# Two layers of a diffusion backbone: sums of token halves moved from the attention's plan behind the first downward blocks, and the first downward tiles split when buffers come free

## The chip, the cores and the metric

The kernel runs on one core of one Trainium2 chip. The metric is the device time of one execution in microseconds. Before the change the median of three runs is 1696.11 us (1695.55 to 1698.88). The engines are named as in the profile: PE is TensorE, DVE is VectorE, ACT is ScalarE, POOL is GpSimd, SP is SyncE, which here issues the weight loads.

## The reference

One inference step of a diffusion backbone: two layers over 128 context tokens and 512 latent tokens (640 in all), width 1024, MLP width 4096. Each layer has an attention part and an MLP part; the change touches the seam between the two.

```python
def rmsnorm(x, g):
    xf = x.astype(jnp.float32)
    y = xf * lax.rsqrt(jnp.mean(xf * xf, axis=-1, keepdims=True) + EPS)
    return (y * g.astype(jnp.float32)).astype(x.dtype)
...
    mix = jnp.concatenate([da_o.reshape(B, S, -1), sw_o.reshape(B, S, -1), mla_o.reshape(B, S, -1)], axis=-1)
    x = x + g1 * (mix @ lw['w_out'])
    h2 = rmsnorm(x, lw['norm2_g']) * (1 + sc2) + sh2
    x = x + g2 * (jnp.square(jax.nn.relu(h2 @ lw['w_up'])) @ lw['w_down'])
    return x, state
```

The four lines from `mix` on close one layer; `mix` joins the outputs of three groups of attention heads. `h2 @ w_up` is the upward projection, the product with `w_down` the downward one. Everything is float32.

## The kernel before, in words

**Precision.** Each operand of a product is kept as a high and a low part in a narrower type that PE reads: `wh` and `wl` for weights, `hh` and `hl` for the normed activations h, `Gt` (both parts in one tile) for the squared relu. The high part is a copy (ACT, L401 or L416), the low part a subtraction of that copy from the raw value (L409, on DVE). A product is three matmuls (L544, L545, L546 in `mm3`; L1483 and L1873 where they are written out): high by high, high by low, low by high. A raw weight tile is `wr`; making `wh` and `wl` from it is called a split.

**Tokens** are worked on in two parts, `hf`=0 (256 tokens: context and the first latents) and `hf`=1 (the other 384).

**The attention plan.** All of the attention and the start of the MLP are tasks of a planner (`Plan`): each has an engine, an estimated length, what it reads and writes, ring buffers to allocate, and a priority (a smaller number goes first). The planner puts the tasks of every engine in a fixed order; on the chip an engine runs its own list in order and waits by semaphores. Rings `wh` and `wl` have four buffers each.

**The end of the plan** in each layer is:
- `emit_h`: h of the second norm, by token part and k (8 pieces of 128 features); `rb` (L681) is a small matmul that spreads the norm's factor over the partitions ahead of it. The value h before its split stays in two tiles `hs` (k 0 to 3 and k 4 to 7).
- `wino_tokens` (L1529): for each token part four subtractions `hs<-hs` of token halves and feature halves, which leave sums of blocks of h in `hs`, then their split into `Th` and `Tl`. These are operands of a scheme of seven products in place of eight that the upward projections use later. The tasks have priority 0.45e6+20; the `Th` copy may go to ACT or DVE as the planner likes ('AV').
- `first_up` (L1473): the upward projection of the first four f-blocks (f=0..3, 128 columns of w_up each). For `hf`=0 (L1483) and then for `hf`=1 (L544 to L546, 384 wide) it loops over k, and within k over all four f. Each f uses one buffer of the rings `wh` and `wl` to its end. Then relu on ACT (L1468), its square on DVE (L1469, named `r`), and the split into `Gt`.
- `pre`: loads and splits of the first two downward tiles, d0 and d1, of priority 3.5e6+4, so their buffers are the ones of f=0 and 1.

**The MLP** behind the plan is written out by hand. `downs(0)` gives eight blocks: for each of four w_down tiles (d0 to d3) one block for `hf`=0 and one for `hf`=1, of 24 matmuls each. Each accumulates in two PSUM banks, which DVE adds to the residual x (L747 in `emit_resid`: 128 wide twice for `hf`=0, 384 wide for `hf`=1). `ups(1)` follows: fourteen blocks (L1873), for two pairs of f-blocks (f=4 and f=6) the seven products A11, A12, S2, S3, S1, A22, S4 in that order; A11, A12 and S4 take h itself, the others `Th` and `Tl`. Their weights are sums of raw tiles that POOL makes (`wr<-wr`, `ws<-wr` at L409, and `pool_late`, L1784).

**What feeds the blocks.** `prep()` splits the next weight tile as soon as the block that used its ring slot last has been issued; it stands at the end of the loop over blocks. Tiles 4 to 7 (two products each: A11 and A12 of f=4; S2 and S3; S1 and A22; then S4 of f=4 with A11 of f=6) are prepared behind blocks 1, 3, 5 and 7. `advance()` then issues the next raw loads on SP: there are four raw buffers, and one is loaded anew once the tiles that read it have been split. When the second raw tile of a pair is there, POOL makes its sums.

```python
                for f_ in now + late:
                    f_()
                late = later
                while state["tile"] < len(tiles) and last_use[state["tile"] - RINGS["wh"]] <= b_:
                    prep()
```

Here `now` holds what empties the PSUM banks of this block, `late` the split of the previous block's `r` into `Gt`.

Of the kernel before, what the change touches and what calls it, by code (L numbers as in the profile page):

```python
# [10 lines left out]
F32 = mybir.dt.float32  # L11
# [47 lines left out]
N_PRE = 2  # L59
# [307 lines left out]
def tile_hybrid_step(ctx: ExitStack, tc: tile.TileContext, i, o):  # L367
    nc = tc.nc
    V, S, G, T = nc.vector, nc.scalar, nc.gpsimd, nc.tensor
# [12 lines left out]
    def mk(ring, shape, dt=F32, name=None):  # L382
        tag = SHARE.get(ring, ring)

        def make():
            pool = psum[ring] if ring in psum else pool_of.get(tag, mp)
            return pool.tile(shape, dt, tag=tag, name=name or ring, bufs=N_RAW if tag == "wr" else RINGS[tag])
        s = Slot(ring, make)
        s.name = name or ring
        return s  # L390

    def add(*a, **k):
        return cur[0].add(*a, **k)
# [5 lines left out]
    def copy(eng, out, in_):  # L399
        if eng is S:  # L400
            S.activation(out=out, in_=in_, func=AF.Copy)  # L401
        else:
            eng.tensor_copy(out, in_)
# [4 lines left out]
    def sub(eng, out, a, b):  # L408
        eng.tensor_tensor(out=out, in0=a, in1=b, op=ALU.subtract)  # L409
# [27 lines left out]
    def sl(t, table, key):  # L437
# [30 lines left out]
                    in1=sil[:, 2].rearrange("p (k s) -> p k s", s=2), op=ALU.mult)  # L468
# [61 lines left out]
    def load_split(src, n, prio, k=1, load_prio=None, after=(), sb=None):  # L530

        raw = load(src, n, prio if load_prio is None else load_prio, after)
        hi, lo = mk("wh", [P, 1024], R), mk("wl", [P, 1024], R)
        split(n, lambda: hi.t[:, :n], lambda: lo.t[:, :n], lambda: raw.t[:, :n], [raw], (hi, lo), prio,
              hi_alloc=[hi], lo_alloc=[lo], sb=sb or PAR["weights"], extra=0.05)

        def view():
            return tuple(s.t[:, :n].rearrange("p (k n) -> p k n", k=k) for s in (hi, lo))

        return view, [hi, lo]  # L540
# [931 lines left out]

    def first_up(l, h, Gt, ws, after):  # L1473

        acc = mk("s", [P, 4, 256], F32, "pu")
        add("V", tV(1024), lambda: V.memset(acc.t, 0.0), alloc=[acc], prio=0.35e6, after=after)
        for k in range(KD):
            for f in range(4):
                def mm(k=k, f=f):
                    wh, wl = ws[f][0]()  # L1480
                    hh, hl = (h_at(h, x, k, slice(*HALVES[0])) for x in "hl")
                    for w, a in ((wh, hh), (wh, hl), (wl, hh)):
                        T.matmul(out=acc.t[:, f], lhsT=w[:, k], rhs=a, start=False, stop=k == KD - 1 and w is wl,  # L1483
                                 skip_group_check=True)

                add("P", 3 * tP(256), mm, r=h_rd(h, k, 0) + ws[f][1], w=[(acc, f)], prio=1.2e6 + 0.1 * k + 0.01 * f)
        acc1 = mk("s", [P, 2, 512], F32, "pu")
        pus = [mk("t", [P, 384], F32, "pu") for _ in range(2)]
        late = [((acc1, f), lambda f=f: acc1.t[:, f, 0:384]) for f in range(2)] + [(x, lambda x=x: x.t) for x in pus]
        for k in range(KD):  # L1490
            for f in range(4):
                key, out = late[f]

                def mm(k=k, f=f, out=out):
                    wh, wl = ws[f][0]()
                    mm3(out(), (wh[:, k], wl[:, k]), [h_at(h, x, k, slice(*HALVES[1])) for x in "hl"], k == 0, k == KD - 1)

                al = [] if k else [[acc1], [], [pus[0]], [pus[1]]][f]
                add("P", 3 * tP(384), mm, r=h_rd(h, k, 1) + ws[f][1], w=[] if al else [key], alloc=al,
                    prio=1.2e6 + 1 + 0.1 * k + 0.01 * f)  # L1500
        for hf in range(2):
            for f in range(4):
                a0, b0 = HALVES[hf]
                w = b0 - a0
                r = mk("E", [P, NT], F32, "r")
                gt = Gt[f // 2]
                d = {}
                pu, out = late[f] if hf else ((acc, f), lambda f=f: acc.t[:, f])

                def stage(x, d=d, gt=gt, f=f, hf=hf, out=out, r=r):  # L1510
                    if "s" not in d:
                        d["s"] = up_out(gt.t, f, hf, out(), r.t)
                    d["s"][x]()

                pr = 0.4e6 + 500 + 4 * hf + f
                add("A", tA(w), lambda stage=stage: stage(0), r=[pu], alloc=[r], prio=pr)
                add("V", tV(w), lambda stage=stage: stage(1), r=[pu], w=[r], prio=pr)
                add("A", tA(w) + 0.05, lambda stage=stage: stage(2), r=[r], w=[(gt, ("h", f, hf))], prio=pr)
                add("V", tV(w), lambda stage=stage: stage(3), r=[r, (gt, ("h", f, hf))], w=[(gt, ("l", f, hf))], prio=pr)
# [4 lines left out]
    def half(ap, x):  # L1524

        return ap.rearrange("p k (t a n) -> p k t a n", a=2, n=64)[:, :, :, x] if len(ap.shape) == 3 else \
            ap.rearrange("p (t a n) -> p t a n", a=2, n=64)[:, :, x]

    def wino_tokens(hs, Tl, Th):  # L1529

        for hf in range(2):
            a, b = HALVES[hf]
            w = (b - a) * 2
            every = [(hs[x], (4 * x + k, hf)) for x in range(2) for k in range(4)]

            def v(s, x, a=a, b=b):
                return half(hs[s].t[:, :, a:b], x)

            for out, in0, in1 in (((0, 0), (0, 1), (0, 0)), ((0, 1), (1, 1), (0, 1)),
                                  ((1, 1), (1, 1), (0, 0)), ((1, 0), (1, 0), (1, 1))):  # L1540
                add("V", tV(w), lambda e=V, v=v, out=out, in0=in0, in1=in1: sub(
                    e, v(*out), v(*in0), v(*in1)), r=every, w=every, prio=0.45e6 + 20)
            for x in (1, 0):
                c = (slice(None), slice(4 * x, 4 * x + 4), slice(a, b))
                n = 4 * (b - a)
                kk = [(4 * x + k, hf) for k in range(4)]
                src = [(hs[x], q) for q in kk]
                sv = lambda x=x, a=a, b=b: hs[x].t[:, :, a:b]
                add("AV", {"A": tA(n), "V": tV2(n)}, lambda e, c=c, sv=sv: copy(e, Th.t[c], sv()),
                    r=src, w=[(Th, q) for q in kk], prio=0.45e6 + 20)  # L1550
                add("V", tV(n), lambda e=V, c=c, sv=sv: sub(e, Tl.t[c], sv(), Th.t[c].bitcast(F32)),
                    r=[(Th, q) for q in kk] + src, w=[(Tl, q) for q in kk], prio=0.45e6 + 20)


    def last_down(l, dn, Gt, st):
# [42 lines left out]
    for l in range(DEPTH + 1):  # L1598
        with ExitStack() as es:
# [17 lines left out]
            if l == 0:  # L1617
                st = open_stats("z")
                for k2 in range(4):
                    add("D", 2 * P * NT * 4 / DMAR, lambda k2=k2: dma(xT[:, 2 * k2:2 * k2 + 2], i["xT"][:, 2 * k2:2 * k2 + 2]),  # L1620
                        w=[("x", (k, hf)) for k in (2 * k2, 2 * k2 + 1) for hf in range(2)], prio=0.0)
# [12 lines left out]
            if l == DEPTH:  # L1634
                for hf in (1, 0):
                    a, b = HALVES[hf]
                    for k in range(KD):
                        def fy(hf=hf, k=k, a=a, b=b):
# [4 lines left out]
                            r=[("x", (k, hf))], prio=0.0)  # L1643
# [21 lines left out]
            for tok in PAR["seq"].split():  # L1665
                kind, u = tok[0], int(tok[1:])
                if kind == "c":
                    for _ in range(u):
                        c = next(conds, None)
# [13 lines left out]
                else:  # L1683
                    n = count[tok] = count.get(tok, -1) + 1
# [22 lines left out]
            Tl, Th = (mk("T", [P, KD, NT], R, n) for n in ("Tl", "Th"))  # L1707
            for x in (Tl, Th):
                x.keep = True
            add("V", 0.0, lambda: None, alloc=[Tl, Th], prio=0.0, after=[gate["mla"]])  # L1710
            hs = [mk("hs", [P, 4, NT], F32, "hs") for _ in range(2)]
            add("V", 0.0, lambda: None, alloc=hs, prio=0.0, after=[gate["mla"]])
            rb2s = rstds(st2, ("o", "t"), 0.3e6, False)
            for hf in range(2):
                for k in range(KD):
                    emit_h(l, 1, hf, rb2s[hf], h2, k, 0.3e6 + 20 * hf + k, hs)
            wino_tokens(hs, Tl, Th)
            upw = []
            for f in range(4):
                upw.append(load_split(i["w_up"][l, f], 1024, PAR["up_prio"] + f, 8, sb=PAR["up"], load_prio=3.5e6 + f))  # L1720
# [12 lines left out]
        with ExitStack() as es:  # L1733
# [10 lines left out]
            Tlt, Tht = Tl.t, Th.t  # L1744
# [91 lines left out]
                return [half(t[:, 4 * x[1]:4 * x[1] + 4], x[2]) for t in (Tht, Tlt)]  # L1836

            banks, late = {}, []
            advance()
            while state["tile"] < RINGS["wh"]:  # L1840
                prep()
            for b_, blk in enumerate(blocks):
                kind, f, q, x, n_ = blk
                wh, wl = wt[n_]
                now, later = [], []
                if kind == "d":
                    g, mc, hf = f, q, x
# [11 lines left out]
                else:  # L1859
# [10 lines left out]
                    out = pu.rearrange("p (t n) -> p t n", n=64)  # L1870
# [4 lines left out]
                    if q in ("A11", "S2", "S3"):  # L1875
                        e = mp.tile([P, 384], F32, tag="X", name="pe", bufs=RINGS["X"])
# [148 lines left out]
```

## Time and profile before

| what | value |
|---|---|
| median of three runs | 1696.11 us |
| the profiled execution, whole | 1699.22 us |
| its span in the trace | 1697.4 us |
| last 128 x 384 matmul of `first_up`, layer 0 / layer 1 | 454.29 / 1274.77 us |
| first upward block behind the eight downward ones, layer 0 / 1 | 490.63 / 1310.21 us |

All times in rows of the trace count from the start of the span. A row of the timeline has start, length, engine, line, operation, output and inputs, size, and in square brackets how long the engine was idle before it and which instruction released it. Matmuls overlap in the pipeline, so their pitch (start to start) is the time that each costs, not the length. "x4" means four instructions in one row, their time added up. Rows of waits give the waiting instruction, what it waited for, total us, count and longest. Line numbers are those of the kernel before; the changed kernel's L1484, L1871, L1881, L1882, L1886 and L1887 are L1483, L1873, L1883, L1884, L1888 and L1889 before.

### The profile page before, as it was taken

What the parts mean: (1) busy time and instruction counts of PE and PEld (TensorE: products, weight loads), DVE (VectorE), ACT (ScalarE), POOL (GpSimd) and SP (SyncE); (2) the same over time, 40 slices, a digit from 0 to 9 for tenths busy, and PEclk for the clock granted to TensorE, in tenths of its full rate; (3) what the DMA queues carried; (4) which work ended last, traced back from release to release, by engine and by line L of the source; (5) the groups of instructions that cost most, each with busy time, mean ns of one, the idle gap of its engine ahead of it and who ended that gap; (6) DMA issues with size and microseconds to landing.
All of it is one profiled execution on the core that took longest, in us unless ns stands there. A gap on an engine that the chain in (4) does not pass through costs nothing.

```text
span 1697.4 us, 29299 instructions
## 1 busy us (share of the span) xinstructions
PE 1612.8 (95%) x11035; PEld 1444.5 (85%) x11035; DVE 1279.2 (75%) x3317; ACT 788.3 (46%) x1771; POOL 202.7 (12%) x164
## 2 busy tenths in 40 slices
PE   6999999998899999999999999989988999999997
PEld 4787668677899999999988766856888999999997
DVE  5875889887968666776596769999896866766666
ACT  4533777774534332343263346776463523433231
POOL 0000002000033122221000000300002322212200
PEclk9999999999899999999999999999999999999998
DMA  9433453532113212232223234124012212221121
GB/s 326 131 91 110 144 173 100 166 103 87 36 63 101 73 53 89 86 100 84 76 63 101 82 111 156 53 91 146 26 63 75 87 63 87 88 100 63 63 75 62
DMA packets 67388, 163.20 MB, mean 96 GB/s; under 512 B 6896, under 2 KB 31280, under 8 KB 67248
## 3 DMA queue, kind: packets, MB, share of 16 engines
q1 hardware_dynamic: 67248, 161.34, 29.1%
q8 instruction: 87, 1.43, 0.3%
q14 instruction: 53, 0.43, 0.1%
HBM read 153.15 MB, written 8.16 MB: 95 GB/s over the span
## 4 chain that ended last, share of the span: by engine, by line
PE 76%; DVE 14%; ACT 4%; DMA 2%; issue 2%; POOL 1%; DVEq 0%; ACTq 0%; SPq 0%; POOLq 0%
PE pu L1873 19%; PE pu L546 8%; PE pu L545 8%; PE pu L544 8%; PE po L544 3%; PE pt L1108 3%; PE O L1122 3%; PE po L546 3%; PE po L545 3%; PE pz L842 3%; PE pz L844 3%; PE pz L843 3%; PE sps L1046 1%; PE pa L578 1%; DVE wl L409 1%
## 5 line engine op out<-in xcount | busy, mean ns | idle before, releaser
L409 DVE TENSOR_TENSOR wl<-wr,wh 128x512 fp32r<-128x512 f32 (+2 forms) x290 | 293.8, 1034 | 58.4 <-ACT wh L416 30.3
L401 ACT ACTIVATE wh<-wr 128x512 fp32r<-128x512 f32 (+1 forms) x228 | 161.0, 736 | 288.8 <-PE pu L545 175.5
L546 PE MATMUL pu<-Gt,wl 128*128 128x384 f32 (+1 forms) x896 | 278.5, 311 | 5.9 <-DVE wl L409 5.9
L544 PE MATMUL pu<-Gt,wh 128*128 128x384 f32 (+1 forms) x896 | 278.3, 311 | 4.3 <-DVE r L1469 4.3
L545 PE MATMUL pu<-Gt,wh 128*128 128x384 f32 (+1 forms) x896 | 278.1, 310 | 0.0
L747 DVE SCALAR_TENSOR_TENSOR xT<-pu,ada,xT 128x128 f32<-128x128 f32 x336 | 134.1, 433 | 142.1 <-PE pu L546 142.0
L546 PEld LDWEIGHTS pu<-Gt,wl 128*128 128x128 f32 x896 | 171.7, 192 | 6.4 <-DVE wl L409 6.4
L544 PEld LDWEIGHTS pu<-Gt,wh 128*128 128x128 f32 x896 | 171.7, 192 | 4.6 <-ACT wh L416 4.6
L545 PEld LDWEIGHTS pu<-Gt,wh 128*128 128x128 f32 x896 | 171.8, 192 | 0.0
L1873 PE MATMUL pu<-Tl,wh 128*128 128x320 f32 x448 | 138.0, 308 | 0.0
L1873 PE MATMUL pu<-Th,wl 128*128 128x320 f32 x448 | 138.0, 308 | 0.0
L1873 PE MATMUL pu<-Th,wh 128*128 128x320 f32 x448 | 138.0, 308 | 0.0
L842 PE MATMUL pz<-wh,hh 128*128 128x512 f32 (+1 forms) x320 | 127.7, 399 | 3.7 <-DVE m L775 1.2
L843 PE MATMUL pz<-wl,hh 128*128 128x512 f32 (+1 forms) x320 | 122.4, 383 | 0.6 <-DVE wl L409 0.6
L844 PE MATMUL pz<-wh,hl 128*128 128x512 f32 (+1 forms) x320 | 122.8, 384 | 0.1
L1060 DVE TENSOR_REDUCE stt<-sps 128x1 f32<-128x640 f32 (+2 forms) x160 | 116.4, 736 | 7.3 <-PE sps L1053 4.2
L1068 ACT ACTIVATE quad<-sps,stt 128x640 f32<-128x640 f32 (+2 forms) x128 | 91.4, 715 | 41.1 <-DVE stt L1060 40.4
L1873 PE MATMUL pu<-hh,wh 128*128 128x320 f32 x336 | 104.2, 310 | 4.3 <-DVE r L1888 4.3
L1873 PE MATMUL pu<-hh,wl 128*128 128x320 f32 x336 | 103.8, 309 | 0.0
L1873 PE MATMUL pu<-hl,wh 128*128 128x320 f32 x336 | 103.6, 308 | 0.0
L1447 POOL TENSOR_TENSOR xT<-xT,tm 128x256 f32<-128x256 f32 (+1 forms) x32 | 33.2, 1040 | 577.8 <-ACT tm L1443 573.6
L409 POOL TENSOR_TENSOR wr<-wr 128x512 f32<-128x512 f32 x28 | 38.3, 1366 | 479.2 <-DMA wr<-in_w_up 326.0
(312 smaller groups left out, 3879.4 us busy)
## 6 DMA issues: line engine op xcount, KB each, us to landing
wr<-in_w_ada SPq DMA_DIRECT2D x80, 512.0 KB, 3.9
wr<-in_w_up SPq DMA_DIRECT2D x64, 512.0 KB, 3.4
wr<-in_w_down SPq DMA_DIRECT2D x64, 512.0 KB, 3.5
wr<-in_w_in SPq DMA_DIRECT2D x24, 512.0 KB, 3.5
wr<-in_w_out SPq DMA_DIRECT2D x16, 512.0 KB, 4.3
wq<-in_w_ada SPq DMA_DIRECT2D x6, 1024.0 KB, 11.6
wr<-in_w_in SPq DMA_DIRECT2D x8, 416.0 KB, 3.7
xT<-in_xT SPq DMA_DIRECT2D x4, 640.0 KB, 6.7
```

The source lines that it names most:

```text
L401: S.activation(out=out, in_=in_, func=AF.Copy)
L409: eng.tensor_tensor(out=out, in0=a, in1=b, op=ALU.subtract)
L544: T.matmul(out=out, lhsT=w[0], rhs=a[0], start=first, stop=False)
L545: T.matmul(out=out, lhsT=w[0], rhs=a[1], start=False, stop=False)
L546: T.matmul(out=out, lhsT=w[1], rhs=a[0], start=False, stop=last)
L747: V.scalar_tensor_tensor(out=xT[:, m, a:b], in0=po[:, a - a0:b - a0], scalar=ada[l][:, sec, m, s:s + 1], in1=xT[:, m, a:b], op0=ALU.mult, ...
L842: T.matmul(out=out, lhsT=h_at(h, "h", k, tk), rhs=wh[:, x], start=(k == 0), stop=False)
L843: T.matmul(out=out, lhsT=h_at(h, "h", k, tk), rhs=wl[:, x], start=False, stop=False)
L844: T.matmul(out=out, lhsT=h_at(h, "l", k, tk), rhs=wh[:, x], start=False, stop=(k == KD - 1))
L1060: add("V", tV(we) - 0.01, lambda st=st, j=j, view=view: V.tensor_reduce(out=st.t[:, j:j + 1], in_=view(), axis=AX.X if kind == "sw" else A ...
L1068: S.activation(out=out, in_=view(), func=AF.Exp, bias=st.t[:, j:j + 1], accum_out=st.t[:, 4 + j:5 + j])
L1873: T.matmul(out=out, lhsT=w_[:, k], rhs=a_[:, k], start=new and k == 0 and y == 0, stop=k == 3 and y == 2, skip_group_check=True)
```

## The change

1. `wino_tokens` no longer adds tasks to the plan. It returns sixteen steps (for each token part four subtractions on DVE, then a copy to `Th` on ACT and a subtraction to `Tl` on DVE for each of the two tiles), and two of them are issued behind each of the first eight downward blocks, ahead of `prep()`. The `Th` copy is always on ACT. `hs` is kept beyond the plan.
2. `first_up` takes f=0 and 1 through all k for `hf`=1, and then f=2 and 3.
3. d0 and d1 are loaded with the old priority but split with priority 0.3e6+100 and up, ahead of the relu of `first_up` where their buffers are free.

```diff
@@ first_up
                 add("P", 3 * tP(384), mm, r=h_rd(h, k, 1) + ws[f][1], w=[] if al else [key], alloc=al,
-                    prio=1.2e6 + 1 + 0.1 * k + 0.01 * f)
+                    prio=1.2e6 + 1 + f // 2 + 0.1 * k + 0.01 * f)
@@ wino_tokens
+        steps = []
         for hf in range(2):
             a, b = HALVES[hf]
...
             for out, in0, in1 in (((0, 0), (0, 1), (0, 0)), ((0, 1), (1, 1), (0, 1)),
                                   ((1, 1), (1, 1), (0, 0)), ((1, 0), (1, 0), (1, 1))):
-                add("V", tV(w), lambda e=V, v=v, out=out, in0=in0, in1=in1: sub(
-                    e, v(*out), v(*in0), v(*in1)), r=every, w=every, prio=0.45e6 + 20)
+                steps.append(lambda v=v, out=out, in0=in0, in1=in1: sub(V, v(*out), v(*in0), v(*in1)))
             for x in (1, 0):
                 c = (slice(None), slice(4 * x, 4 * x + 4), slice(a, b))
-                add("AV", {"A": tA(n), "V": tV2(n)}, lambda e, c=c, sv=sv: copy(e, Th.t[c], sv()),
-                    r=src, w=[(Th, q) for q in kk], prio=0.45e6 + 20)
-                add("V", tV(n), lambda e=V, c=c, sv=sv: sub(e, Tl.t[c], sv(), Th.t[c].bitcast(F32)),
-                    r=[(Th, q) for q in kk] + src, w=[(Tl, q) for q in kk], prio=0.45e6 + 20)
+                sv = hs[x][:, :, a:b]
+                steps.append(lambda c=c, sv=sv: copy(S, Th[c], sv))
+                steps.append(lambda c=c, sv=sv: sub(V, Tl[c], sv, Th[c].bitcast(F32)))
+        return steps
@@ the end of the plan
             hs = [mk("hs", [P, 4, NT], F32, "hs") for _ in range(2)]
+            for x in hs:
+                x.keep = True
...
-            wino_tokens(hs, Tl, Th)
...
-            pre = [load_split(i["w_down"][l, 0, mc], 1024, 3.5e6 + 4 + mc, 4)[1] for mc in range(N_PRE)]
+            pre = [load_split(i["w_down"][l, 0, mc], 1024, 0.3e6 + 100 + mc, 4, load_prio=3.5e6 + 4 + mc)[1] for mc in range(N_PRE)]
@@ the blocks
+            sums = wino_tokens([x.t for x in hs], Tlt, Tht)
...
                 late = later
+                for f_ in sums[2 * b_:2 * b_ + 2]:
+                    f_()
                 while state["tile"] < len(tiles) and last_use[state["tile"] - RINGS["wh"]] <= b_:
                     prep()
```

How the order on the engines changes is shown at three places. The first is DVE at the end of layer 0's plan, before: from the `Gt` of the first token part to the first residuals (`128x1024` of `wl` are the tiles d0 to d3).

```order
L409 TENSOR_TENSOR Gt<-r,Gt 128x256 x3
L409 TENSOR_TENSOR Tl<-hs,Th 128x4x256
L409 TENSOR_TENSOR hs<-hs 128x4x3x64 x4
L403 CAST Th<-hs 128x4x384
L409 TENSOR_TENSOR Tl<-hs,Th 128x4x384 x2
L1469 SCALAR_TENSOR_TENSOR r<-pu,r 128x384 x4
L409 TENSOR_TENSOR Gt<-r,Gt 128x384 x4
L409 TENSOR_TENSOR wl<-wr,wh 128x1024 x4
L747 SCALAR_TENSOR_TENSOR xT<-pu,ada_92,xT 128x128 x4
```

The same place on DVE with the change, up to the end of block 1's work:

```order
L409 TENSOR_TENSOR Gt<-r,Gt 128x256 x3
L409 TENSOR_TENSOR wl<-wr,wh 128x1024 x2
L1469 SCALAR_TENSOR_TENSOR r<-pu,r 128x384 x2
L409 TENSOR_TENSOR Gt<-r,Gt 128x384 x2
L1469 SCALAR_TENSOR_TENSOR r<-pu,r 128x384 x2
L409 TENSOR_TENSOR Gt<-r,Gt 128x384 x2
L409 TENSOR_TENSOR wl<-wr,wh 128x1024 x2
L747 SCALAR_TENSOR_TENSOR xT<-pu,ada_92,xT 128x128 x4
L409 TENSOR_TENSOR hs<-hs 128x4x2x64 x2
L747 SCALAR_TENSOR_TENSOR xT<-pu,ada_92,xT 128x384 x2
L409 TENSOR_TENSOR hs<-hs 128x4x2x64 x2
```

The splits of d0 and d1 stand ahead of the square relu of `hf`=1, those of d2 and d3 behind it, and the sums are gone from here to the blocks.

The second place is DVE around blocks 6 and 7 (residuals of tile d3) and the split of tile 7 behind them, in layer 0, with the change; the two rows with `Tl` are the last steps of the sums.

```order
L409 TENSOR_TENSOR wl<-wr,wh 128x512 x2
L747 SCALAR_TENSOR_TENSOR xT<-pu,ada_92,xT 128x128 x4
L409 TENSOR_TENSOR Tl<-hs,Th 128x4x384
L747 SCALAR_TENSOR_TENSOR xT<-pu,ada_92,xT 128x384 x2
L409 TENSOR_TENSOR Tl<-hs,Th 128x4x384
L409 TENSOR_TENSOR wl<-wr,wh 128x512 x2
L1886 TENSOR_TENSOR r<-pu,pe 128x320
```

Before, the same rows stood there without the two `Tl`.

The third place is PE in `first_up` of layer 0, with the tiles' numbers: the first matmuls of `hf`=1 (wh_4976, wh_5124, wh_5244 are the high parts of f=0, 1 and 2). Before:

```order
L544 MATMUL pu_5500<-hh0_5291,wh_4976 128x384
L545 MATMUL pu_5500<-hl0_5293,wh_4976 128x384
L546 MATMUL pu_5500<-hh0_5291,wl_4992 128x384
L544 MATMUL pu_5500<-hh0_5291,wh_5124 128x384
L545 MATMUL pu_5500<-hl0_5293,wh_5124 128x384
L546 MATMUL pu_5500<-hh0_5291,wl_5142 128x384
L544 MATMUL pu_5513<-hh0_5291,wh_5244 128x384
```

With the change:

```order
L546 MATMUL pu_5499<-hh0_5291,wl_4992 128x384
L544 MATMUL pu_5499<-hh0_5291,wh_5124 128x384
L545 MATMUL pu_5499<-hl0_5293,wh_5124 128x384
L546 MATMUL pu_5499<-hh0_5291,wl_5142 128x384
L544 MATMUL pu_5499<-hh0_5291,wh_4976 128x384
```

After f=1 the same two f-blocks go on with the next k; f=2 comes after all eight k, 48 matmuls from the start of `hf`=1. Ahead of this part, the three `rb` matmuls of `hf`=1 moved up by 21 rows on PE in layer 0, from among the L1483 matmuls of a later k; in layer 1 they stand where they stood.

More of the change, by code (lines that the diff above doesn't have):

```diff
@@ L1529, in wino_tokens @@
     def wino_tokens(hs, Tl, Th):
+        steps = []
         for hf in range(2):
             a, b = HALVES[hf]
-            w = (b - a) * 2
-            every = [(hs[x], (4 * x + k, hf)) for x in range(2) for k in range(4)]
             def v(s, x, a=a, b=b):
-                return half(hs[s].t[:, :, a:b], x)
+                return half(hs[s][:, :, a:b], x)
             for out, in0, in1 in (((0, 0), (0, 1), (0, 0)), ((0, 1), (1, 1), (0, 1)),
                                   ((1, 1), (1, 1), (0, 0)), ((1, 0), (1, 0), (1, 1))):
-                add("V", tV(w), lambda e=V, v=v, out=out, in0=in0, in1=in1: sub(
-                    e, v(*out), v(*in0), v(*in1)), r=every, w=every, prio=0.45e6 + 20)
+                steps.append(lambda v=v, out=out, in0=in0, in1=in1: sub(V, v(*out), v(*in0), v(*in1)))
             for x in (1, 0):
                 c = (slice(None), slice(4 * x, 4 * x + 4), slice(a, b))
[L1545 to L1548, printed above, removed]
-                add("AV", {"A": tA(n), "V": tV2(n)}, lambda e, c=c, sv=sv: copy(e, Th.t[c], sv()),
-                    r=src, w=[(Th, q) for q in kk], prio=0.45e6 + 20)
-                add("V", tV(n), lambda e=V, c=c, sv=sv: sub(e, Tl.t[c], sv(), Th.t[c].bitcast(F32)),
-                    r=[(Th, q) for q in kk] + src, w=[(Tl, q) for q in kk], prio=0.45e6 + 20)
+                sv = hs[x][:, :, a:b]
+                steps.append(lambda c=c, sv=sv: copy(S, Th[c], sv))
+                steps.append(lambda c=c, sv=sv: sub(V, Tl[c], sv, Th[c].bitcast(F32)))
+        return steps
     def last_down(l, dn, Gt, st):
```

## The prediction

> **What bounds the kernel now.** I read the page's busy line first, then the chain that ended last, then PE's waits in the two stretches that the change touches (the end of each layer's attention plan and its first downward blocks).
>
> ```profile
> span 1697.4 us, 29299 instructions
> PE 1612.8 (95%) x11035; PEld 1444.5 (85%) x11035; DVE 1279.2 (75%) x3317; ACT 788.3 (46%) x1771; POOL 202.7 (12%) x164
> PE 76%; DVE 14%; ACT 4%; DMA 2%; issue 2%; POOL 1%; DVEq 0%; ACTq 0%; SPq 0%; POOLq 0%
> ```
>
> TensorE (PE) works 95% of the span, so only PE's idle time, or time at a lower clock, can be won. No matmul is added or removed. The next view is PE's waits, layer 0 (416 to 520 us) and then layer 1 (1236 to 1345 us); columns are total, count, longest.
>
> ```profile
> PE pu L546 <- DVE wl L409: 5.7, 1, 5.7
> PE pu L1873 <- DVE r L1888: 2.0, 2, 1.8
> ...
> PE pu L544 <- DVE r L1469: 4.3, 1, 4.3
> PE pu L1873 <- DVE r L1888: 2.4, 2, 1.9
> ```
>
> Each layer has one long wait on DVE at the first downward block and a short one in the upward blocks behind it. The sums sit ahead of the first:
>
> ```profile
> 447.21 3.93 DVE L409 TENSOR_TENSOR hs<-hs 128x768 f32<-128x768 f32 x4
> 452.18 3.43 DVE L409 TENSOR_TENSOR Tl<-hs,Th 128x1536 fp32r<-128x1536 f32 x2
> 459.25 4.62 DVE L409 TENSOR_TENSOR wl<-wr,wh 128x1024 fp32r<-128x1024 f32 x4
> ...
> 453.90 1.61 ACT L1468 ACTIVATE r<-pu 128x384 f32<-128x384 f32 x4
> ...
> 1276.85 0.55 DVE L1469 SCALAR_TENSOR_TENSOR r<-pu,r 128x384 f32<-128x384 f32 x1
> ```
>
> DVE works without a gap from 447 to 463 us: sums first, and the low parts `wl` of the downward tiles last.
>
> **The gain.** These PE rows are the end of `first_up` (L546 with 384 columns), the wait, and the first matmuls of blocks 0 to 3; even blocks are 256 wide, odd ones 384.
>
> ```profile
> 454.29 0.33 PE L546 MATMUL pu<-hh,wl 128*128 128x384 f32 x1
> 460.53 0.58 PE L546 MATMUL pu<-Gt,wl 128*128 128x256 f32 x1 [5.66 <-DVE wl L409]
> 465.34 0.34 PE L544 MATMUL pu<-Gt,wh 128*128 128x384 f32 x1
> 469.53 0.28 PE L544 MATMUL pu<-Gt,wh 128*128 128x256 f32 x1
> 472.39 0.34 PE L544 MATMUL pu<-Gt,wh 128*128 128x384 f32 x1
> ...
> 1274.77 0.34 PE L546 MATMUL pu<-hh,wl 128*128 128x384 f32 x1
> 1279.42 0.55 PE L544 MATMUL pu<-Gt,wh 128*128 128x256 f32 x1 [4.31 <-DVE r L1469]
> 1284.94 0.34 PE L544 MATMUL pu<-Gt,wh 128*128 128x384 f32 x1
> ```
>
> An undisturbed even block takes 472.39 - 469.53 = 2.86 us, an odd one 469.53 - 465.34 = 4.19 us. So a pair is 7.05 us, and the first eight blocks are 28.2 us.
>
> Layer 0: the split of tiles d0 and d1 now waits only for the raw tiles and for the last matmuls of f=0 and 1, which with the new order of f lie half of the 384-wide part, some 8 us, before the end of `first_up`. Both splits stand ahead of the last r on DVE, so they are done by then. Block 0 follows `first_up` at about 454.47 (0.17 us, one pitch, after its last matmul), and block 1 at 454.47 + 2.86 = 457.33 instead of 465.34: **8.0 us** earlier. That is the wait of 5.66 and what block 0 lost at a low clock, below. What is late next is nothing in this place: the Gt of the first half are made before the splits.
>
> Layer 1: the wait there is for the last r (a PSUM bank), and the bank still has to be emptied. Without sums ahead of it, it costs one ACT relu (1.61 / 4 = 0.40) and one DVE step (0.55) behind the end of `first_up` at 1275.1: block 0 starts near 1276.2, block 1 at 1279.1 instead of 1284.94, **5.8 us** earlier. A wait of 1 us stays. Together -13.8.
>
> The risk in `first_up` itself: each k-step of f=0,1 now takes half the time, so the second half of h is wanted sooner. The row of rb that feeds it moves ahead on PE in layer 0, and the sums that delayed h on DVE are gone, so I cost this at nothing; if h were late, each k would cost up to 1 us (half of four 384-wide groups).
>
> **The cost: DVE in the first eight blocks.** The sums are not removed. Here is what DVE and POOL do there before: residuals L747 beside their waits for PE, and splits with and without POOL at work.
>
> ```profile
> 467.65 0.62 DVE L747 SCALAR_TENSOR_TENSOR xT<-pu,ada,xT 128x384 f32<-128x384 f32 x1 [1.50 <-PE pu L546]
> 470.26 3.04 DVE L409 TENSOR_TENSOR wl<-wr,wh 128x512 fp32r<-128x512 f32 x2
> 473.23 1.11 DVE L747 SCALAR_TENSOR_TENSOR xT<-pu,ada,xT 128x128 f32<-128x128 f32 x4
> 484.35 1.29 DVE L409 TENSOR_TENSOR wl<-wr,wh 128x512 fp32r<-128x512 f32 x2
> ...
> 465.40:486.00 20.60, 20.60 (x142) 20.60 (x142) 12.33 (x24) 3.46 (x6) 8.51 (x6) 1.00 0.14 55
> ```
>
> The last row is a window: its length, then busy time and count of PE, PEld, DVE, ACT, POOL, then the granted clock. DVE had 12.33 of 20.6 us in use. Now, from the split of d2 to the first half of tile 7's split, DVE has to do: splits of d2 and d3 4.62 / 2 = 2.31; residuals 4 x 1.11 and 8 x 0.62 = 9.40; the sums of the first 256 tokens 4 x 0.65 (a 512-wide subtraction, 1.29 / 2) = 2.60, and of the other 384 tokens 3.93; Tl 2 x 1.16 (1024 wide) and 3.43; splits of tiles 4 to 6 3 x 1.29 and half a tile 0.65. In all 2.31 + 9.40 + 2.60 + 3.93 + 2.31 + 3.43 + 4.52 = **28.5 us, against 28.2 us of blocks**. Th goes to ACT, which had 3.46 of 20.6 us in use, and I cost it at nothing.
>
> On top comes contention: two 512-wide splits took 3.04 us while POOL subtracted and 1.29 while it did not, 1.75 us more. Residuals, which read PSUM, are no slower beside it (1.11 for four). POOL has 8.51 us there, now with SBUF subtractions beside most of it. I take 2.5 us; the bounds are 0 and 8.51 x (1 - 1.29 / 3.04) = 4.9.
>
> [...]
>
> Who waits for this is shown by the chain of waits of layer 1 (start, length, engine, line):
>
> ```profile
> 1310.57 0.64 ACT wh L401
> 1311.23 0.70 DVE wl L409
> 1311.95 3.60 DMA wr<-in_w_up
> 1315.71 1.65 POOL wr L409
> 1317.44 1.46 POOL ws L409
> 1318.90 1.72 POOL wr L1784
> 1320.64 0.64 ACT wh L401
> 1321.30 1.07 DVE wl L409
> 1322.38 0.41 DVE r L1888
> 1322.83 9.07 PE pu L1873 x60
> ```
>
> Tile 7's first half (S4 of f=4) is the last reader of a raw buffer. Its split, right behind block 7, releases the next load on SP's queue; three POOL subtractions, a copy, a split and the r behind it on DVE follow, and PE waits for that r. So each microsecond that this split is late is one more in the wait of 1.8 or 1.9 us. The program now puts block 7's two sum steps, a Tl of 1.71 us (3.43 / 2) among them, ahead of it: **1.7 us at the least** in each layer.
>
> Layer 0: DVE turns to d2 near 457.0 (454.5 + relu 0.4 + two r and two Gt of 0.49 each). Without a stop 457.0 + 28.5 + 2.5 = 488.0, while block 7 ends at 454.5 + 28.2 = 482.7: 5.3 us behind. Before, that distance was some 1.5 us (in the chain, 1311.93 against a copy that starts behind PE at 1310.57). Delay **+3.8**, bounds 1.7 and (with 4.9 of contention) 6.2. Layer 1: block 0 itself waits for r, so DVE has a start of 1.3 us more: **+2.5**, bounds 1.7 and 4.9.
>
> The waits then are 1.8 + 3.8 = 5.6 and 1.9 + 2.5 = 4.4 us. Does the clock fall in them? Windows of before (same columns):
>
> ```profile
> 454.90:460.50 5.60, 0.00 (x0) 0.00 (x0) 5.60 (x11) 5.09 (x9) 0.00 (x0) 0.82 0.00 0
> 460.50:465.20 4.70, 4.67 (x22) 4.67 (x23) 3.90 (x5) 0.00 (x0) 0.00 (x0) 0.50 0.70 201
> 501.30:503.10 1.80, 0.04 (x1) 0.00 (x0) 1.77 (x3) 0.00 (x0) 0.81 (x1) 1.00 0.00 0
> ...
> 1275.20:1279.40 4.20, 0.00 (x0) 0.01 (x1) 4.20 (x9) 3.28 (x8) 0.00 (x0) 0.79 0.00 0
> 1279.40:1284.50 5.10, 4.81 (x21) 4.53 (x22) 5.10 (x7) 2.32 (x3) 0.00 (x0) 0.50 0.53 152
> ```
>
> A mean of 0.82 over 5.6 us with half speed at the end means that the clock fell 3.6 us into that wait (0.36 x 5.6 = 2.0 at half); 0.79 over 4.2 us means 2.4 us into the other. Behind the wait it stayed at 0.50 for 4.7 to 5.1 us, in which PE does half its work, a loss of up to 2.4 us. Waits of 1.8 did not do it. So both new waits should lose it: 1.9 each (1.5 to 2.4), **+3.8**. The second wait of each layer, 2.0 - 1.8 = 0.2 and 2.4 - 1.9 = 0.5 us, goes, as PE arrives later: taken as -0.5.
>
> **Sum:** -13.8 + 3.8 + 2.5 + 3.8 - 0.5 = **-4.2 us**. The profiled execution took 1699.22 us (1.8 outside its span), 3.1 over the median, so it would be 1695.0; against the median, 1696.11 - 4.2 = **1691.9**.
>
> **Rivals.** *DVE keeps up.* Its gaps of 1.5 us in the blocks and little overlap with POOL leave only the 1.7 us of one Tl: -13.8 + 3.4 - 0.5 = -10.9, 1685.2; waits of 3.5 us may or may not lose the clock, 1689.0 if both do; middle 1687. For it: 28.5 against 28.2 is even. Against: DVE starts 2.5 us late in layer 0, and 8.5 us of POOL lie beside.
>
> *The clock falls in one of the waits only.* It fell 3.6 us into one wait and 2.4 into the other; if it takes 3.6 and more here, layer 1's 4.4 us lose little: 1691.9 - 1.9 = 1690.0. [...] The fall after 2.4 us speaks against it.
>
> *DVE becomes the bound* (the slower side). With 4.9 us of contention the delays are 6.2 and 4.9, the clock loses 2.4 twice: -13.8 + 11.1 + 4.8 - 0.5 = +1.6, 1697.7. It is slower than before once the two delays exceed 13.8 + 0.5 - 4.8 = 9.5 us together, and by over 0.2% (3.4 us, about what a measurement of this kernel can tell from no change) from 12.9. For it: DVE has no reserve there. Against: before, the same POOL work cost it 1.75 us.
>
> *The change doesn't do what it says:* d0 and d1 get split late after all, because the raw tile or h is late, and the gain of 13.8 shrinks to what the costs are: about 1696. The waits in the program speak against it.
>
> **How the numbers follow.** Forecast 0.50 (1689.5 to 1694.5 by its own bounds); DVE keeps up 0.22; one fall 0.10; DVE the bound 0.11; no effect 0.07. Faster by over 0.2% (under 1692.7) holds three fifths of the forecast and both cheaper rivals, 0.60 in round numbers; slower (over 1699.5) a bit less than half of the bound case, 0.05; the rest, 0.35, is within. The range from 1686.5 to 1697.0 leaves out the low end of the second case and most of the bound case.
>
> **What would show it.** Right: no wait on `wl` at the first block of layer 0 and one of about 1 us on r in layer 1; DVE without gaps in the first eight blocks; the wait on r L1886 behind S1 grown to 4.4 to 5.6 us, with clock 0.5 behind it. Wrong: a wait on h inside `first_up`; DVE gaps that stay, and the grown wait near 3.5 us; or a PE wait inside the first eight blocks.

## The result and the profile after

The changed kernel takes 1688.4 us in the median of 12 runs (1684.81 to 1694.92), against 1699.04 for the kernel before (12 runs, 1695.55 to 1703.92): a ratio of 0.9941, interval 0.9927 to 0.9956. That is faster by 0.6%, some 10 us. The forecast was 4.2 us. The sign and the range held, and the size was under half of what came.

PE's waits of the changed kernel in the same two stretches (405 to 520 us and 1220 to 1345 us), against 5.7 and 4.3 us at the first block before:

```profile
PE pu L1871 <- DVE r L1886: 4.0, 2, 3.2
...
PE pu L1871 <- DVE r L1886: 3.5, 2, 3.0
...
PE pu L544 <- DVE r L1469: 1.2, 1, 1.2
```

The wait on `wl` is gone in layer 0, the one on r in layer 1 is 1.2 us, and the wait on r at S4 of f=4 grew from 1.8 and 1.9 to 3.2 and 3.0. To see what each is worth, the same matmuls are laid beside one another in the two traces. PE rows of the changed kernel: the norm's matmul ahead of the change, the start of block 1, S4 of f=4, S4 of f=6, for layer 0 and then for layer 1.

```profile
415.28 2.72 PE L663 MATMUL st<-cst,sq 128*128 128x1 f32 x12 [3.52 <-DVE sq L655]
454.94 0.34 PE L544 MATMUL pu<-Gt,wh 128*128 128x384 f32 x1
494.15 0.63 PE L1871 MATMUL pu<-hh,wh 128*128 128x320 f32 x1 [3.24 <-DVE r L1886]
508.79 0.41 PE L1871 MATMUL pu<-hh,wh 128*128 128x320 f32 x1 [0.76 <-DVE r L1886]
1230.16 1.50 PE L663 MATMUL st<-cst,sq 128*128 128x1 f32 x12 [0.27 <-DVE sq L655]
1272.21 0.34 PE L544 MATMUL pu<-Gt,wh 128*128 128x384 f32 x1
1311.15 0.41 PE L1871 MATMUL pu<-hh,wh 128*128 128x320 f32 x1 [2.96 <-DVE r L1886]
1324.26 0.43 PE L1871 MATMUL pu<-hh,wh 128*128 128x320 f32 x1 [0.53 <-DVE r L1886]
```

The same rows of the kernel before, without the two block 1 rows shown already (465.34 and 1284.94):

```profile
417.33 2.62 PE L663 MATMUL st<-cst,sq 128*128 128x1 f32 x12 [3.51 <-DVE sq L655]
503.11 0.41 PE L1873 MATMUL pu<-hh,wh 128*128 128x320 f32 x1 [1.77 <-DVE r L1888]
515.89 0.41 PE L1873 MATMUL pu<-hh,wh 128*128 128x320 f32 x1 [0.20 <-DVE r L1888]
1237.47 1.50 PE L663 MATMUL st<-cst,sq 128*128 128x1 f32 x12 [0.27 <-DVE sq L655]
1322.83 0.41 PE L1873 MATMUL pu<-hh,wh 128*128 128x320 f32 x1 [1.91 <-DVE r L1888]
1335.86 0.41 PE L1873 MATMUL pu<-hh,wh 128*128 128x320 f32 x1 [0.46 <-DVE r L1888]
```

| matmul | before | after | difference | step | forecast |
|---|---|---|---|---|---|
| ahead of the change, layer 0 | 417.33 | 415.28 | -2.05 | -2.05 | not the change |
| block 1, layer 0 | 465.34 | 454.94 | -10.40 | -8.35 | -8.0 |
| S4 of f=4 | 503.11 | 494.15 | -8.96 | +1.44 | +3.8 |
| S4 of f=6 | 515.89 | 508.79 | -7.10 | +1.86 | +1.9 clock; second waits of both layers -0.5 |
| ahead of the change, layer 1 | 1237.47 | 1230.16 | -7.31 | -0.21 | |
| block 1, layer 1 | 1284.94 | 1272.21 | -12.73 | -5.42 | -5.8 |
| S4 of f=4 | 1322.83 | 1311.15 | -11.68 | +1.05 | +2.5 |
| S4 of f=6 | 1335.86 | 1324.26 | -11.60 | +0.08 | +1.9 clock |

The last difference is that of the spans, 1697.4 - 1685.8 = 11.6 us. The first 2 us of it belong to the two executions and not to the change. Most of them arise at 25 us into the program, long before it, where this execution of the kernel before ran its matmuls at a low clock (window, columns as before),

```profile
24.60:28.60 4.00, 3.93 (x10) 2.88 (x10) 3.42 (x11) 1.98 (x5) 0.00 (x0) 0.57 1.02 403
```

and the profiled one of the changed kernel didn't (that of experiment 1 below, which also has the change, did: 0.57 too):

```profile
24.60:28.60 4.00, 4.00 (x29) 2.51 (x29) 3.42 (x11) 2.21 (x5) 0.00 (x0) 1.00 1.02 402
```

The steps from block 1 of layer 0 on, without the -0.21 between the layers, add up to -9.3 us, which agrees with the ratio (10 us, 7.5 to 12.4 by its interval).

**Where the cost came out smaller.** DVE of the changed kernel, from the split of d2 and d3 through the two splits beside POOL to the split of tile 7:

```profile
454.95 2.36 DVE L409 TENSOR_TENSOR wl<-wr,wh 128x1024 fp32r<-128x1024 f32 x2
461.97 3.51 DVE L409 TENSOR_TENSOR wl<-wr,wh 128x512 fp32r<-128x512 f32 x2
481.84 1.75 DVE L409 TENSOR_TENSOR Tl<-hs,Th 128x1536 fp32r<-128x1536 f32 x1
483.51 1.29 DVE L409 TENSOR_TENSOR wl<-wr,wh 128x512 fp32r<-128x512 f32 x2
```

The chain of waits from the end of tile 7's first half on:

```profile
484.22 3.35 DMA wr<-in_w_up
487.69 1.30 POOL wr L409
489.07 1.64 POOL ws L409
490.71 1.23 POOL wr L1781
491.96 0.64 ACT wh L401
492.62 1.07 DVE wl L409
```

DVE has no gap from 454.95 to the end of tile 7's first half at 484.20: 29.2 us, where 28.5 + 2.5 = 31.0 were forecast. Block 7 ends at 480.2, so the end of that half is 4.0 us behind it, against 1.5 before and 5.3 forecast. From the end of that split to S4 it is 494.15 - 484.20 = 9.95 us; before it was 503.11 - 492.07 = 11.04 (the split of 491.38 was half done at 492.07). So +2.5 of lag and -1.1 of chain make the +1.44.

Last, the clock at S4 of f=4, layer 0 and layer 1:

```profile
491.00:494.15 3.15, 0.00 (x0) 0.00 (x0) 1.50 (x3) 0.63 (x1) 2.15 (x2) 0.92 0.00 0
494.15:499.00 4.85, 4.85 (x24) 4.85 (x25) 3.87 (x8) 2.31 (x5) 0.00 (x0) 0.70 0.31 98
1308.20:1311.15 2.95, 0.00 (x1) 0.01 (x1) 1.50 (x3) 0.63 (x1) 1.94 (x2) 1.00 0.00 0
1311.15:1316.00 4.85, 4.85 (x33) 4.85 (x34) 3.97 (x9) 3.35 (x8) 0.00 (x0) 1.00 0.31 88
```

It fell in layer 0 alone, 24 matmuls in 4.85 us in place of 33, which is the +1.3 in the step of 1.86; the other 0.56 is the second wait, 0.20 before and 0.76 now.

### The profile page after: what moved, and what is told of

It reads as the page before. It is cut to its first block, busy times and chain, and to the rows that moved or that the text cites. A ratio compares the mean times of both kernels' runs of the same rounds, so it can differ in the third digit from the quotient of the medians.

```text
span 1685.8 us, 29293 instructions
## 1 busy us (share of the span) xinstructions
PE 1609.4 (95%) x11035; PEld 1443.1 (86%) x11035; DVE 1270.1 (75%) x3315; ACT 792.7 (47%) x1773; POOL 204.0 (12%) x164
## 3 DMA queue, kind: packets, MB, share of 16 engines
q8 instruction: 87, 1.43, 0.3%
## 4 chain that ended last, share of the span: by engine, by line
PE 76%; DVE 14%; ACT 3%; DMA 2%; issue 2%; POOL 0%; DVEq 0%; SPq 0%; ACTq 0%; POOLq 0%
PE pu L1871 19%; PE pu L544 8%; PE pu L545 8%; PE pu L546 8%; PE po L544 3%; PE pt L1108 3%; PE O L1122 3%; PE po L546 3%; PE po L545 3%; PE pz L842 3%; PE pz L844 3%; PE pz L843 3%; DVE wl L409 2%; PE pu L1484 2%; PE pa L578 1%
## 5 line engine op out<-in xcount | busy, mean ns | idle before, releaser
L409 DVE TENSOR_TENSOR wl<-wr,wh 128x512 fp32r<-128x512 f32 (+2 forms) x290 | 289.3, 1018 | 68.0 <-ACT wh L401 34.2
L544 PEld LDWEIGHTS pu<-Gt,wh 128*128 128x128 f32 x896 | 169.8, 190 | 1.6 <-DVE r L1469 1.6
L545 PEld LDWEIGHTS pu<-Gt,wh 128*128 128x128 f32 x896 | 169.9, 190 | 0.0
```

The source lines that it names most:

```text
L544: T.matmul(out=out, lhsT=w[0], rhs=a[0], start=first, stop=False)
L545: T.matmul(out=out, lhsT=w[0], rhs=a[1], start=False, stop=False)
```

## The experiments

Times are medians; the kernel before took 1698.6 to 1699.6 us beside these runs. Differences to the changed kernel that are called "aligned" come from laying the same matmuls of the two traces side by side, as above: from the start of block 1 (in experiment 3, which changes `first_up` too, from the norm's matmul ahead of it) to the place behind the upward blocks from which the two run in step.

**1. One Tl more ahead of tile 7's split.** The question is whether the wait at S4 follows that split one for one.

```diff
                 for f_ in sums[2 * b_:2 * b_ + 2]:
                     f_()
+                if b_ == 7:
+                    sums[15]()
```

> The changed kernel with the last Tl step issued twice, 1.7 us more on DVE ahead of tile 7's split, in both layers. Theory A: waits 4.9 and 4.7 us, the clock falls in both and costs about 2 us each, +3.4 + 2.7 = about +6 us against the changed kernel. Theory B (DVE has slack there): waits within 0.5 us of 3.2 and 3.0, time the same.

It took 1693.18 us (ratio 0.9968, 0.9954 to 0.9983). Waits of layer 0 and layer 1:

```profile
PE pu L1871 <- DVE r L1886: 5.6, 2, 4.8
...
PE pu L1871 <- DVE r L1886: 4.9, 2, 4.2
```

On DVE of layer 0 the two Tl stand in one row ahead of the split, which starts at 485.18:

```profile
481.72 3.54 DVE L409 TENSOR_TENSOR Tl<-hs,Th 128x1536 fp32r<-128x1536 f32 x2
```

That is 3.46 us in place of 1.67. For 1.8 us more on DVE the waits grew by 1.6 and 1.2 us. Theory A is right in its path, at a slope of 0.7 to 0.9 and not of one. Aligned, layer 0 lost 2.2 us and layer 1 3.0 (the clock now fell there too, at 1315.39 us).

**2. Split first, sums behind.** If the last Tl costs 1.7 us, it should be won back by putting it behind the split.

```diff
-                for f_ in sums[2 * b_:2 * b_ + 2]:
-                    f_()
                 while state["tile"] < len(tiles) and last_use[state["tile"] - RINGS["wh"]] <= b_:
                     prep()
+                for f_ in sums[2 * b_:2 * b_ + 2]:
+                    f_()
```

> The changed kernel with prep ahead of the two sum steps behind each block, so that the last Tl (1.75 us) stands behind tile 7's split. Theory A (the wait follows the start of tile 7's split one for one): waits 3.2 - 1.7 = 1.5 and 3.0 - 1.7 = 1.3 us, clock at 1.00, -1.7 - 1.3 - 1.7 = -4.7 us against the changed kernel. Theory B (POOL's contention or DVE's whole load sets it): waits stay over 2.5 us, gain under 1.5 us.

It took 1691.18 us (0.9948, 0.9929 to 0.9966), no better than the changed kernel; the waits were 3.1 and 3.3 us. DVE of this kernel:

```profile
460.46 3.50 DVE L409 TENSOR_TENSOR hs<-hs 128x512 f32<-128x512 f32 x2
465.22 2.23 DVE L409 TENSOR_TENSOR Tl<-hs,Th 128x1024 fp32r<-128x1024 f32 x1 [0.22 <-ACT Th L401]
479.40 1.76 DVE L409 TENSOR_TENSOR Tl<-hs,Th 128x1536 fp32r<-128x1536 f32 x1 [0.52 <-ACT Th L401]
482.13 1.28 DVE L409 TENSOR_TENSOR wl<-wr,wh 128x512 fp32r<-128x512 f32 x2
```

The expectation of theory A fell. The Tl was out of the way, but POOL's subtractions now met two of DVE's operations, the sums (3.50 us where two take 1.41 without POOL) and a Tl (2.23 for 1.26), and Th came late on ACT because its copies stood behind the tile's: 0.7 us of gaps. What DVE won by the order it lost again. It also made S2, which needs Tl, wait for 0.8 us in layer 0. Aligned, 3.5 us were lost, 0.8 of them in that wait; where the rest went, no row here shows, and the intervals of the medians overlap.

**3. Each part of the change alone.** First the early split and the order of f without the moved sums:

> The kernel before with the early split of d0 and d1 and the new order of f; the sums stay in the plan. Theory A (the first wait is the late split, the sums matter little once it is early): no wait on wl at block 0 of layer 0, but Gt of f=2,3 and tile d2 behind the sums cost about 1 us each; gain 5 to 6 us in layer 0 and about 4 in layer 1, and the wait on r at S4 stays at 1.8 to 1.9. Theory B (the sums must go): waits of 4 us and more stay in the first blocks, gain under 3 us in all.

One execution, 1691.31 us. Its two first waits:

```profile
456.84 0.45 PE L545 MATMUL pu<-Gt,wh 128*128 128x384 f32 x1 [1.60 <-DVE Gt L409]
1272.18 0.58 PE L544 MATMUL pu<-Gt,wh 128*128 128x256 f32 x1 [6.27 <-DVE r L1469]
```

Each theory holds in one layer. In layer 0 the early split is all of it: 1.6 us of wait on Gt, but S4's wait stays at 1.8 and block 0 doesn't wait; aligned, layer 0 is 0.8 us faster than with the whole change. In layer 1 the last r stands behind Th and Tl on DVE, and block 0 waits 6.3 us, longer than before; aligned, 6.1 us slower than the whole change.

Then the moved sums alone:

> The changed kernel with the old priority of d0's and d1's split and the old order of f; only the sums are moved. Theory A: d0's split comes at the end of first_up and d1's behind r and Gt, so waits of 1 to 2 us stay at block 0 and again within blocks 0 to 2 in each layer, 2 to 4 us lost of the 13.8; the wait at S4 as in the changed kernel, 3.0 to 3.3. Theory B (the sums' move alone does it): under 0.7 us of waits in the first blocks of layer 0.

One execution, 1698.46 us, no gain. Neither theory fits both layers. Block 0 of layer 1 waits as in theory A, for longer than it priced, and S4 of layer 0 waits longer than the 3.3 us it gave. The rows are S4 in layer 0 and block 0 in layer 1:

```profile
498.71 0.63 PE L1871 MATMUL pu<-hh,wh 128*128 128x320 f32 x1 [5.34 <-DVE r L1886]
1277.05 0.55 PE L544 MATMUL pu<-Gt,wh 128*128 128x256 f32 x1 [4.06 <-DVE r L1469]
```

The first blocks of layer 0 waited 0.4 us only, as theory B has it, but three of the four downward splits stood behind r and Gt, so DVE went into the blocks later still and S4 waited 5.3 us.

And the whole change with the old order of f:

```diff
-                    prio=1.2e6 + 1 + f // 2 + 0.1 * k + 0.01 * f)
+                    prio=1.2e6 + 1 + 0.1 * k + 0.01 * f)
```

> The changed kernel with the old order of f in first_up (k outermost, all four f). Theory A (the order is what lets the buffers of f=0,1 come free early): d0 and d1 are split only behind first_up's end, and ahead of the last r on DVE: waits of about 1 us on wl at block 0 of layer 0 and 3 us on r in layer 1, +3 to +5 us against the changed kernel. Theory B (the priority alone does it): no more than 0.5 us of new waits.

One execution, 1704.27 us. The rows are S4 in layer 0 and block 0 in layer 1:

```profile
499.11 0.64 PE L1871 MATMUL pu<-hh,wh 128*128 128x320 f32 x1 [4.83 <-DVE r L1886]
1280.10 0.55 PE L544 MATMUL pu<-Gt,wh 128*128 128x256 f32 x1 [5.20 <-DVE r L1469]
```

Theory A is right that the order matters, but far more is lost than the 3 to 5 us it expected, and in layer 0 it is lost at S4 and not on `wl` at block 0 (0.4 us). Without this line the splits of d0 and d1 come at the end of `first_up` and ahead of the last r, where they are in the way: the early split doesn't pay then, since without both it was 1698.46. Aligned, the old order costs 6.2 us in layer 0 and 10.2 in layer 1. In it are clock falls (0.50 over the 4.9 us behind each of the rows above, and one more at S4 of layer 1, where the pitch of its 320-wide matmuls went from 0.15 to 0.27 us) and waits of 1.2 us on ACT's `pe`.

All four kernels against the kernel before, aligned, one execution each:

| kernel | layer 0 | layer 1 |
|---|---|---|
| the whole change | -5.0 | -4.3 |
| early split and new order of f, sums in the plan | -5.9 | +1.8 |
| moved sums alone | -0.2 | +1.5 |
| moved sums and early split, old order of f | +1.2 | +5.9 |

The new order of f without the early split was not run.

**4. What holds the r at S4?** Two queues could: POOL's, where `pool_late` of f=6 stands behind the subtractions for f=8 that wait for loads, and DVE's, where r stands behind a split that waits for POOL. First POOL's order:

```diff
                         if b_:
-
-                            r0, r1 = p["r"]
-                            sub(G, r1[:, lo_], r0[:, lo_], r1[:, lo_])
-                            p["ws"] = psum["ws"].tile([P, 512], F32, tag="ws", name="ws", bufs=RINGS["ws"])
-                            sub(G, p["ws"], r1[:, hi_], r1[:, lo_])
+                            if a_ == 8:
+                                held.append(p)
+                            else:
+                                pair_subs(p)
...
                         if q == "A12":
                             pool_late(p)
+                            while f == 6 and held:
+                                pair_subs(held.pop())
```

> The changed kernel, but POOL's two subtractions for the pair f=8 are issued behind pool_late of f=6 instead of ahead of it. Theory A (the wait at block S4 of f=4 is POOL's queue: pool_late of f=6 stands behind subtractions that wait for loads, which wait for tile 7's split): both waits of 3.2 and 3.0 us fall under 0.5 us and the clock stays at 1.00 there, -3.2 - 1.3 (clock) - 3.0 = -7.5 us against the changed kernel, about 1681 us, less what comes late next (the second wait, 0.8 and 0.5 us, may grow by 1 each). Theory B (DVE itself is too far behind after the sums): waits of 1.5 us or more stay, gain under 3.5 us.

It took 1684.03 us (0.9912, 0.9894 to 0.9931), with waits of 2.2 and 1.4 us, between the theories. DVE and POOL in layer 0:

```profile
485.95 1.58 DVE L409 TENSOR_TENSOR Gt<-r,Gt 128x320 fp32r<-128x320 f32 x1
487.46 3.44 DVE L409 TENSOR_TENSOR wl<-wr,wh 128x512 fp32r<-128x512 f32 x2
...
487.15 1.54 POOL L409 TENSOR_TENSOR wr<-wr 128x512 f32<-128x512 f32 x1
```

And two windows of layer 0, the first with the whole wait in it:

```profile
488.92:492.33 3.41, 1.22 (x8) 0.97 (x7) 3.34 (x6) 0.47 (x2) 1.43 (x1) 1.00 0.00 0
492.33:495.74 3.41, 3.41 (x15) 3.41 (x14) 2.92 (x6) 1.85 (x5) 0.00 (x0) 0.50 0.29 79
```

`pool_late` no longer waits for a load, and POOL no longer holds the r. The second queue still does: POOL's subtractions now run against DVE's, a Gt takes 1.58 us for 0.49 and the two splits ahead of r 3.44 for 1.29. And the clock fell behind this wait of 2.2 us. Aligned it gained 2.0 us; the medians say more, but their intervals touch.

The same with the sums behind the splits as in 2:

> As pool_order, and prep stands ahead of the two sum steps behind each block. Theory A: within 0.5 us of pool_order, since the split of tile 7 no longer gates anything PE waits for. Theory B: 1.7 us a layer below pool_order, as one Tl less is ahead of tile 7's split.

1688.77 us (0.9936, 0.9916 to 0.9956), waits of 2.6 and 2.6 us. Neither theory expected it to be worse than `pool_order`; the traces show a longer wait, and what in the order of the sums caused it wasn't taken apart.

Then DVE's order:

```diff
-                while state["tile"] < len(tiles) and last_use[state["tile"] - RINGS["wh"]] <= b_:
+                while state["tile"] < len(tiles) and last_use[state["tile"] - RINGS["wh"]] + (state["tile"] == 9) <= b_:
```

> The changed kernel with tile 9 (S3 and S1 of f=6) prepared behind block 12 instead of block 11, so that on DVE the r of S1 of f=4 stands ahead of the split that waits for POOL. Theory A (PE's wait is that r standing in DVE's queue behind a split that isn't ready): both waits of 3.2 and 3.0 us go to under 0.5, the clock stays up there, -3.2 - 1.3 - 3.0 = -7.5 us against the changed kernel, near 1681 us; the second wait (0.8, 0.5) grows by at most 1. Theory B (DVE's whole lag): r itself is late, waits of 1.5 us or more stay.

It took 1686.6 us (0.9927, 0.9911 to 0.9943). Both waits at S4 of f=4 are gone, and the clock stays up (1.00 from 490 to 520 and from 1305 to 1335 us), as theory A has it. But behind it PE waits three times in each layer; layer 0:

```profile
504.06 0.42 PE L1871 MATMUL pu<-Th,wh 128*128 128x320 f32 x1 [0.78 <-ACT pe L401]
507.01 0.42 PE L1871 MATMUL pu<-hh,wh 128*128 128x320 f32 x1 [0.93 <-DVE r L1886]
513.19 0.41 PE L1871 MATMUL pu<-Th,wh 128*128 128x320 f32 x1 [0.64 <-ACT pe L401]
```

So the cause of the wait is shown: it is the r standing in DVE's queue behind a split that isn't ready. Of the 7.5 us, aligned, 3.5 stay (by the medians it is not clear of the changed kernel); the rest comes back as waits on ACT's copies `pe` and on the next r, since POOL's chain is as late as it was: its first subtraction starts 5.9 us behind the start of the last Tl of layer 0 in both kernels.

Both together:

> pool_order and late9 together. Theory A (two queues hold the r of S1: POOL's loads ahead of pool_late, and DVE's split ahead of r): no wait at S4 of f=4 in either layer, and none on ACT's pe behind it, since the copy that blocked ACT no longer waits for POOL; the second wait stays at 0.8 to 1.0. That is -3.2 - 1.3 - 3.0 + 0.6 = about -6.9 us against the changed kernel, near 1681 us. Theory B (the lost time only moves on): waits of 2 us or more in all appear behind it in each layer, gain under 4 us.

```profile
505.23 0.41 PE L1881 MATMUL pu<-hh,wh 128*128 128x320 f32 x1 [0.96 <-DVE r L1896]
511.40 0.41 PE L1881 MATMUL pu<-Th,wh 128*128 128x320 f32 x1 [0.63 <-ACT pe L401]
...
1320.32 0.41 PE L1881 MATMUL pu<-hh,wh 128*128 128x320 f32 x1 [1.51 <-DVE r L1896]
```

Theory A holds in the main, 1 us short: no wait at S4 of f=4, but in layer 0 a wait of 0.6 us on `pe` that it ruled out, and in layer 1 a second wait of 1.5. It took 1683.37 us, ratio 0.9906 (0.9891 to 0.9921), about 6 us under the changed kernel (0.9927 to 0.9956), and aligned 5.9. It beats both kernels.

One step further with the next r:

> As pool_late9, and tile 12 is prepared two blocks later too, so that the r of S1 of f=6 stands ahead of its split on DVE. Theory A: the second wait of 0.8 to 1.0 goes as well, -1.6 us against pool_late9. Theory B: what stands behind the later split is late in its place; no gain over pool_late9.

1682.54 us (0.9911, 0.9896 to 0.9927): no gain over the last one. The wait on r went, and a wait on ACT's `pe` of 2.2 us in layer 0 and 1.6 in layer 1 took its place, as theory B said. In the trace it is 1.9 us behind the last one, aligned, mostly because the clock fell behind the wait of 2.2 (0.83 from 505 to 515 us, where the last one had 1.00).

## Why the prediction was right in its steps and off in its size

- **The gain: right.** -8.35 and -5.42 us against -8.0 and -5.8. The 1.2 us that stay in layer 1 are the relu and r that were named. What the prediction did not separate is which part of the change earns it: experiment 3 shows that in layer 0 the early split with the new order of f does, and the moved sums cost some 0.8 us; in layer 1 the sums must go too.
- **h in time: right.** Neither trace stretch shows a wait on h in the second half of `first_up`.
- **"Layer 0: ... Delay +3.8", "+2.5": right in mechanism, too large.** They came to 1.44 and 1.05, below the 1.7 that was called the least. Two sizes were off. The lag of tile 7's split was 4.0 us and not 5.3, mostly since lengths were added that overlap, some 0.07 us from row to row. The length of a row "x2" or "x4" runs from the start of its first instruction to the end of its last and is not their time added up, as was said ahead of the prediction; but one row still overlaps the next. The rows of that stretch add up to 30.9 us and took 29.2. For instance, two 384-wide residuals take 1.05 us from their start to that of the next row (473.97 to 475.02), where 2 x 0.62 was counted. The extra for POOL was 2.2 us, in one place (3.51 for 1.29), near the 2.5 taken, so that term held. And the chain from that split to S4 was taken as fixed, "one more in the wait for each microsecond"; it got 1.1 us shorter in layer 0 and 0.4 in layer 1. POOL's three subtractions took 4.2 us in it for 4.6 and 4.9 before, and in layer 0 the split behind them took 0.5 us less (1.07 for 1.53; POOL's next subtraction lay beside 0.5 us of it for 1.0); the load took 0.3 us less in layer 0 and 0.2 more in layer 1. Experiment 1 gives the slope by itself: 0.7 to 0.9.
- **"So both new waits should lose it", 3.8 us: wrong by two thirds.** The waits were shorter than forecast, 3.2 and 3.0 us, and the clock cost 1.3 us in layer 0 and nothing in layer 1. By the estimate of the last section waits of 5.6 and 4.4 us would have lost it in both, and at 3.2 and 3.0 us it is luck where the wait lies, so the 1.3 us are those of this execution.
- **The second waits, -0.5: wrong in sign.** They grew from 0.20 to 0.76 and from 0.46 to 0.53. That PE comes later doesn't take them away: the last run of experiment 4 shows that they too are an r behind a split (tile 12's). Why they grew was not taken apart.
- **The sum.** Of the 5 us between -4.2 and the -9.3 of the traces, 3.8 are the two delays and 1.4 the clock with the second waits; the gain was right to 0.1.
- **The rivals.** "DVE keeps up", 1685 to 1689, is nearest in its time, but not in its reason: DVE had no gap in the eight blocks of layer 0, and one of 0.6 us in layer 1. Of its result, the smaller delay and one clock fall, the size came from the overlap, the shorter chain and a wait that kept the clock by its place.

## What to carry to other kernels

Ask of a stall which instruction stands at the head of the queue ahead of the one that is waited for. Here the r was ready and stood behind a split that waited for POOL, and one move of that split in issue order took away the whole wait. But a stall that goes shows the next: about half of what that move won came back on ACT and on the next r a few microseconds later, so a gain has to be measured behind the place and not at it. When a cost is summed from rows of a trace, take starts of successive rows and not their lengths; and the lines of a change should be priced in their combinations, since here an early split lost time without the matmul order that frees its buffers. And the clock can fall in one execution and not in another at the same place, as at 25 us above (0.57 and 1.00), so a step read from one trace each should be compared with the medians.

## What the runs showed of the hardware that was not expected

In these traces how long PE waits doesn't decide alone whether the clock falls; its place in time does too. In each of the twelve traces all changes of the granted clock lie whole steps of 3.41 us apart. In the kernel before, for instance, the clock goes down at 24.94 and at 458.43 us, 127 such steps apart, and up at 28.35 and 465.26. Cut the trace into slices by these steps and take PE's idle time in each, from the second half of `first_up` to the end of the upward blocks, in both layers of all twelve traces. All 17 slices at full clock in which PE idled 1.97 us or more were followed by half speed; none with 1.73 us or less was, and none lies between. So the wait of 2.2 us with POOL's order changed, which lay in one slice (the two windows in experiment 4), lost the clock. The wait of 3.0 us in layer 1 of the changed kernel was cut in two, 1.22 and 1.73 us, and kept it:

```profile
1306.00:1309.41 3.41, 2.19 (x15) 1.93 (x14) 0.53 (x1) 0.46 (x1) 3.35 (x3) 1.00 0.00 0
1309.41:1312.83 3.42, 1.68 (x11) 1.69 (x12) 3.15 (x6) 1.35 (x4) 0.73 (x1) 1.00 0.00 0
```

The wait of 4.2 us in layer 1 of experiment 1 was cut into 1.43 and 2.74, and the clock fell at the end of the second slice, at 1315.39, when PE had begun again at 1314.72. The falls that the prediction read as 3.6 and 2.4 us into a wait are ends of slices too (458.43 and 1277.63). An estimate from these slices, for these stretches: a wait of over 3.9 us (2 x 1.97) loses the clock wherever it lies, one of under 1.7 never, and one between by its place. In the rest of the program the two groups overlap: falls come from 0.83 us of idle on, and some slices with up to 1.65 us have none. So idle time in the trace isn't all that counts, and what else does stays open.

DVE and POOL slowed each other in these runs: beside POOL's subtractions two 512-wide splits took 3.44 to 3.51 us for 1.29, one Gt 1.58 for 0.49, and a subtraction on POOL 2.27 for 1.29 (at 466.60 in the changed kernel; the Tl beside it took 1.28, the next, almost clear of POOL, 1.26). What makes them do so, no row shows.
